# A decoder block on one core: short waits of later stages, and the order of the products in front

## The chip, the cores and the metric

The kernel runs on one core of a Trainium2 chip. Its engines are TensorE (PE in the profile), VectorE (DVE), ScalarE (ACT), GpSimd (POOL) and SyncE (SP), which issues most of the DMAs. Each engine works through its own list of instructions, and semaphores tie the lists together. The metric is the time of one execution on the device in microseconds, the median of several runs.

## What is computed

One layer of a decoder block on a sequence of 1024 positions of width 1024, in float32. Cut to what matters:

```python
mod = silu(c) @ w_ada + b_ada
shift, scale, gate = split(mod, 3)
h = rms_norm(x, norm_gain) * (1 + scale) + shift
q, k, v, z_a, u, z_b, m_a, m_b = split(h @ w_in)
p_a = (stick_breaking_attention(q, k, v) * silu(z_a)) @ w_branch_a
p_b = (multiscale_causal_pool(u, pool_w, pool_scale) * silu(z_b)) @ w_branch_b
merged = sigmoid(m_a) * p_a + sigmoid(m_b) * p_b
y = x + gate * (merged @ w_out)
out = rms_norm(y, final_gain)
```

Attention has 16 heads of 64; each weight is a sigmoid of a logit times the product of (1 - sigmoid) over the later keys before the query. The pooling branch has four groups of 256 channels, each with a trailing window and a linear map of its own.

## The kernel before

**Precision.** A float32 product is made of three products of fp32r operands (a rounded type): operand = high part + low part, and high x high, high x low and low x high are added in one PSUM bank. The high part is a copy into fp32r (`copy_to`, mostly a CAST on ACT), the low part the subtraction operand - high (on DVE as a rule, on POOL for some weights). `load_w` (line 125) loads a weight tile of 512 KB and splits it, `split` (line 110) does the two steps. Product number three of each row block is the first that needs the low part of the weights.

**Stages.** In front, until about 45 us, c goes through silu, the modulation vectors are made on DVE (`modulation`, instructions named mj, 1024 wide, two for each of 8 blocks of h), x is normalised and turned on PE (`square_x`, `scale_x`, `turn_x`) and h is written as high and low (`make_h` on ACT, `low_h` on DVE). Meanwhile PE multiplies the weights of u with the pooling maps (`mapped`: instructions wm, results wg): group g, quarters q 0 to 3. Groups up to `WHOLE` use the plain float32 operands, the later ones fp32r parts. `spread` copies the row c to all partitions with two products with one weight row (crow), and a sigmoid on ACT and a product on DVE give silu(c) there (scb). Then `ua` adds up the first four outputs of u over 8 blocks kb: for each block the eight products with h high (needing `make_h`), later the four with h low (needing `low_h`). Then come v, the pooling branch (wzb, pb), attention with the other projections (z, wt, av, p), and the end, `fin`: for each half `sh` of the sequence eight products pa (attention x w_branch_a, index j), combined on DVE with the gates read back from DRAM (s, m, b: `m*b`, `s<-pa,s`, `m+s`, then high and low parts mhl), then four row blocks o (x w_out), and the last norm (y, qq, t).

**Order.** In front the order is written out by hand: while `pinned` is set, `order(...)` keeps an instruction in the place where the code issues it. Later stages leave the order within an engine to the scheduler of the tile layer, which places instructions by its own estimate of when they can start; so a change of a buffer count can move instructions of a whole stage. PE takes its list in order, and so does DVE: what stands behind a waiting instruction waits too. DMAs of SP are issued in the order of its list, each when its buffer is free. Tags give buffers: `s_`, `m_`, `b_` have 2 each, so a load for index j waits for the user of index j-2. Weights have 2 raw and 2 split buffers (`raw`, `whl`).

**Names.** `ua_273<-hT,wg_143` is output ua from operands hT and wg; numbers behind a name only number buffers. In pa, wa, s, m, b and mhl the digit is the index j.

Of the kernel before, what the change touches and what calls it, by code (L numbers as in the profile page):

```python
# [15 lines left out]
P = 128  # L16
# [20 lines left out]
PLAIN = 8  # L37
LO_V = (1, 0, 1, 1, 0, 1, 1, 0)
# [8 lines left out]
WHOLE, G2 = 2, 1  # L47
# [8 lines left out]
def block_kernel(ctx, tc, a, out):  # L56
# [7 lines left out]
    big = ctx.enter_context(pool("big"))  # L64
    wts = ctx.enter_context(pool("wts"))
# [15 lines left out]
    ident = const.tile([P, P], F32, name="ident")  # L81
    make_identity(nc, ident)
    ones = const.tile([P, P], F32, name="ones")
# [54 lines left out]
    def make_lo(pl, n, tag=None, bufs=3):  # L138

        for _ in range(n):  # L140
# [7 lines left out]
            act.copy(hi, raw)  # L148
            v.tensor_sub(raw.bitcast(F32R), raw, hi.bitcast(F32))
            nc.sync.dma_start(wl_d[i], raw)  # L150

    def load_parts(i, name):
        if i < PLAIN:
            return load_w(a["w_in"][tiles[i]], name, act, gp)
# [47 lines left out]
    with pool("init") as init:  # L202
# [3 lines left out]

        crow = init.tile([P, D], F32, tag="vjunk", bufs=1, name="crow")[0:1]
# [7 lines left out]
        def spread():  # L215
            crows = [bank("tr", f"crow{hf}") for hf in range(2)]
            for hf in range(2):
                mm(crows[hf], ones[0:1, :], crow[:, hf * 512:hf * 512 + 512], start=True, stop=True)
            for hf in range(2):
                sigb = init.tile([P, 512], F32, tag="hf", bufs=2, name=f"sigb{hf}")  # L220
                order(act.activation)(sigb, crows[hf], AF.Sigmoid)
                order(v.tensor_mul)(scb[:, hf * 512:hf * 512 + 512], crows[hf], sigb)
# [18 lines left out]
        def square_x(sb):  # L241
# [3 lines left out]
            gp.tensor_tensor(st[:, 2:3], st[:, 0:1], mhalf[:, 0:1], op=ALU.pow)  # L245

# [33 lines left out]

        def turn_x(sh, kb):
            pt = xts[sh, kb] = bank(("tr", "av")[kb % 2], f"xt{sh}_{kb}")
            for i in range(4):
                transpose(pt[:, i * P:(i + 1) * P], xs[4 * sh + i][:, kb * P:(kb + 1) * P])
# [19 lines left out]
        wg, maps, halves = {}, {}, {}  # L304
# [11 lines left out]
        def split_map(g):  # L316
            hl = init.tile([P, 2, 2, 256], F32R, tag="phl", bufs=1, name=f"phl{g}")
            order(act.copy)(hl[:, 0], maps[g])
            order(v.tensor_sub)(hl[:, 1], maps[g], hl[:, 0].bitcast(F32))
            maps[g] = hl  # L320
# [7 lines left out]
        def mapped(g, q, tag):  # L328
# [4 lines left out]
            th, ml = halves[g, q // 2], maps[g]  # L333
            for e in range(2):
                ks = slice((2 * q + e) % 4 * P, (2 * q + e) % 4 * P + P)

                pairs = [(th[:, cb, ks], ml[:, cb]) for cb in range(2)] if g < WHOLE else [
                    (th[:, i, cb, ks], ml[:, j, cb]) for i, j in ((0, 0), (0, 1), (1, 0)) for cb in range(2)]
                for n, (l, r) in enumerate(pairs):
                    mm(ps[:, e * 256:e * 256 + 256], l, r, start=n == 0, stop=n == len(pairs) - 1)  # L340

            def out(which=(0, 1)):
# [3 lines left out]
                if 1 in which:  # L346
                    order(v.tensor_sub)(dst[:, 1], ps, dst[:, 0].bitcast(F32))
            return out
# [16 lines left out]
        load_mod(0, [slice(1, 2)])  # L365
        load_half(1, 1, t1[:, 1])
        load_x(3)
        load_mod(1)
# [23 lines left out]
        m11 = mapped(1, 1, "pj")  # L392
        modulation(0, (1,))
# [688 lines left out]
```

## Time and profile before

| what | value |
|---|---|
| median of 3 runs | 1212.78 us (1212.56 to 1213.09) |
| the profiled execution, its own time | 1212.4 us |
| its span, first to last instruction | 1210.4 us |
| PE busy | 1199.6 us, 99% of the span |
| DVE, ACT, POOL busy | 757.9, 540.6, 193.8 us |
| mean granted TensorE clock | 0.999 |

PE busy and the span differ by 10.8 us, and the time outside the span is 2.0 us. The profile's timeline gives for each run of equal instructions the start, the time from the first start to the last end, the engine, line and operation, output<-inputs, shapes and count, and in brackets the idle time of that engine before it with what ended it. Ends of PE instructions are modelled: a row block's 512 columns are listed as 0.39 us long but follow one another faster.

### The profile page before, as it was taken

How to read it: one execution, taken by the hardware profiler on the slowest of the kernel's cores; microseconds unless marked ns; L12 is line 12 of the kernel's file. 1: busy time of each engine (PE TensorE's matmuls, PEld its weight loads, DVE VectorE, ACT ScalarE, POOL GpSimd, SP SyncE). 2: the span in 40 equal slices, each digit the busy share in tenths (PEclk: the TensorE clock that was granted, in tenths of full speed). 3: DMA queues.
4: the chain of work that ended last, by engine and by line, in shares of the span. 5: the costliest groups of instructions: out<-in, count | busy, mean ns of one | idle time of the engine just before them, and what ended most of it. 6: DMA issues, size and time to landing. Idle time of an engine off the chain costs nothing.

```text
span 1210.4 us, 16174 instructions
## 1 busy us (share of the span) xinstructions
PE 1199.6 (99%) x5746; PEld 1000.1 (83%) x5746; DVE 757.9 (63%) x1049; ACT 540.6 (45%) x1008; POOL 193.8 (16%) x361
## 2 busy tenths in 40 slices
PE   8999999999999999999999999999999999999997
PEld 7888888888888888888888888888888888888886
DVE  6764482677410277767768677776777763785643
ACT  5564341334211265665556655655655653232211
POOL 1000000001222343212212122231211310000001
PEclk9999999999999999999999999999999999999999
DMA  9649994626846632442635325353343236984622
GB/s 361 255 168 339 326 383 167 214 82 230 317 148 117 179 92 75 133 121 78 170 109 157 113 80 153 109 158 115 106 132 102 96 126 211 315 275 168 218 65 84
DMA packets 81955, 207.13 MB, mean 171 GB/s; under 512 B 10450, under 2 KB 23890, under 8 KB 79699
## 3 DMA queue, kind: packets, MB, share of 16 engines
q1 hardware_dynamic: 73666, 191.23, 49.2%
q10 hardware_dynamic: 8208, 14.88, 3.3%
q8 instruction: 45, 0.74, 0.2%
q14 instruction: 36, 0.29, 0.1%
HBM read 138.96 MB, written 50.34 MB: 156 GB/s over the span
## 4 chain that ended last, share of the span: by engine, by line
PE 93%; DVE 2%; DMA 2%; issue 1%; ACT 0%; POOL 0%; SPq 0%; POOLq 0%; DVEq 0%; ACTq 0%
PE p L99 36%; PE pb L99 7%; PE wzb L99 7%; PE v L99 7%; PE o L99 6%; PE av L99 6%; PE z L99 6%; PE wt L99 5%; PE pa L99 5%; PE u L99 5%; PE ua L99 3%; PE wm L99 1%; DMA m<-sb_d 1%; DMA out_y<-y 0%; DMA praw<-in_pool_w 0%
## 5 line engine op out<-in xcount | busy, mean ns | idle before, releaser
L99 PE MATMUL p<-hT,w 128*128 128x512 f32 x1920 | 480.9, 392 | 0.0
L99 PEld LDWEIGHTS p<-hT,w 128*128 128x128 f32 x1920 | 354.8, 188 | 68.6
L804 DVE TENSOR_TENSOR_SCAN om<-om 128x512 f32<-128x512 f32 (+7 forms) x128 | 175.4, 1370 | 50.0 <-ACT om L797 41.5
L824 DVE TENSOR_TENSOR wt<-wt,wt 128x512 fp32r<-128x512 f32 (+1 forms) x160 | 100.5, 628 | 93.7 <-ACT wt L823 93.1
L823 ACT CAST wt<-wt 128x512 fp32r<-128x512 f32 (+1 forms) x160 | 87.5, 547 | 130.2 <-PE wt L99 129.7
L797 ACT ACTIVATE om<-z 128x512 f32<-128x512 f32 (+2 forms) x192 | 94.9, 494 | 77.2 <-PE z L99 52.2
L802 POOL TENSOR_SCALAR_AFFINE_SELECT om<-om 128x128 f32<-128x128 f32 x128 | 50.9, 397 | 364.3 <-ACT om L797 344.0
L99 PE MATMUL av<-wt,vv 128*128 128x512 f32 x320 | 106.0, 412 | 0.0
L99 DVE TENSOR_TENSOR be<-be,om 128x511 f32<-128x511 f32 (+7 forms) x128 | 95.8, 758 | 0.3
L798 ACT ACTIVATE be<-z 128x512 f32<-128x512 f32 (+2 forms) x192 | 94.2, 491 | 0.0
L99 PE MATMUL pa<-ga,wa 128*128 128x512 f32 x384 | 89.9, 390 | 0.3 <-DVE s L976 0.2
L99 PEld LDWEIGHTS wt<-ident,be 128*128 128x128 f32 x576 | 72.7, 140 | 20.9
L99 PE MATMUL o<-wo,mhl 128*128 128x512 f32 (+1 forms) x408 | 89.6, 377 | 0.0
L99 PE MATMUL wt<-ident,be 128*128 128x128 f32 x576 | 88.7, 272 | 0.0
L99 PE MATMUL v<-wv,hT 128*128 128x512 f32 x384 | 87.2, 389 | 0.0
L99 PE MATMUL wzb<-hT,wzb 128*128 128x512 f32 x384 | 87.2, 389 | 0.0
L99 PE MATMUL pb<-gb,wb 128*128 128x512 f32 x384 | 87.2, 389 | 0.0
L99 PEld LDWEIGHTS o<-wo,mhl 128*128 128x128 f32 x408 | 73.5, 188 | 14.1
L99 PEld LDWEIGHTS pa<-ga,wa 128*128 128x128 f32 x384 | 71.9, 188 | 15.9 <-issue 0.6
L99 PEld LDWEIGHTS v<-wv,hT 128*128 128x128 f32 x384 | 72.1, 188 | 14.9
L99 PEld LDWEIGHTS wzb<-hT,wzb 128*128 128x128 f32 x384 | 72.1, 188 | 14.9
L99 PEld LDWEIGHTS pb<-gb,wb 128*128 128x128 f32 x384 | 72.1, 188 | 14.9
(129 smaller groups left out, 1374.2 us busy)
## 6 DMA issues: line engine op xcount, KB each, us to landing
w_raw<-in_w_in SPq DMA_DIRECT2D x40, 512.0 KB, 4.8
l_raw<-in_w_in SPq DMA_DIRECT2D x32, 512.0 KB, 5.1
wl_d<-l_raw SPq DMA_DIRECT2D x32, 512.0 KB, 5.8
w<-wl_d SPq DMA_DIRECT2D x32, 512.0 KB, 3.9
v_d<-vo SPq DMA_DIRECT2D x16, 512.0 KB, 4.8
vv<-v_d SPq DMA_DIRECT2D x8, 1024.0 KB, 5.5
wa_raw<-in_w_branch_a SPq DMA_DIRECT2D x16, 512.0 KB, 4.8
wa<-in_w_mod SPq DMA_DIRECT2D x7, 1024.0 KB, 6.5
```

What stands on the lines that cost most here:

```text
L99: ins = op(*args, **kw)
L797: act.activation(om[:, b0:b0 + n], zp[:, :n], AF.Sigmoid, scale=-0.125)
L798: act.activation(be[:, b0:b0 + n], zp[:, :n], AF.Sigmoid, scale=0.125)
L802: gp.affine_select(out=tl[:, :P], in_=tl[:, :P], pattern=[[1, P]], compare_op=ALU.is_gt, fill=fill, base=0, channel_multiplier=-1)
L804: v.tensor_tensor_scan(om[:, :W], om[:, :W], om[:, :W], 1.0, ALU.mult, ALU.min)
L823: act.copy(wt[:, 0, :off], pt[:, :off])
L824: v.tensor_sub(wt[:, 1, :off], pt[:, :off], wt[:, 0, :off].bitcast(F32))
```

## The change

1. Front. `ident` and `ones` get a pool of their own, which moves them in memory. A sigmoid on a tile of 8 columns runs first on ACT, with the tile set again by POOL. `spread` is split in two halves, each between `mapped` quarters; quarters 2 and 3 of group 0 use fp32r parts (`WHOLE` is now a table of halves), for which the map and the second half of the weights are split (`cast_map`, `low_map`, `cast`). The scaling of row block 0 goes from DVE to ACT (`scale_act`). The half (1,1) of the weights and x block 3 are loaded ahead of the second half of the first modulation weights. Quarters 2 and 3 of group 1 use banks "av" and "tr", the latter with its second part behind the turning of x, and their low parts come later.
2. The low part of one weight tile of attention (number 4, `MASKED`) goes from POOL to DVE.
3. In the v stage the work on weights to be stored and on the pooling differences is issued one step later than its loads (`later`, `load_u`). The rows of every engine stand there as before.
4. In `fin` the buffers of s, m and b go from 2 to 3.

```diff
-WHOLE, G2 = 2, 1
+WHOLE = ((0, 0), (1, 0), (1, 1))
+MASKED = 4
...
     def load_parts(i, name):
         if i < PLAIN:
-            return load_w(a["w_in"][tiles[i]], name, act, gp)
+            return load_w(a["w_in"][tiles[i]], name, act, v if i == MASKED else gp)
...
+        act.activation(mhalf, mhalf, AF.Sigmoid)
+        gp.memset(mhalf, -0.5)
...
+        def scale_act(sb):
+            order(act.mul)(xs[sb], xs[sb], stats[sb][:, 2:3])
...
         load_mod(0, [slice(0, 1)])
         load_x(2)
-        load_mod(0, [slice(1, 2)])
         load_half(1, 1, t1[:, 1])
         load_x(3)
+        load_mod(0, [slice(1, 2)])
...
-        mapped(0, 0, "pj")()
+        m00 = mapped(0, 0, "pj")
+        cast_map(0)
+        low_map(0)
+        m00()
+        t0_lo = cast(0, 1)
+
+        spread(0)
         m01 = mapped(0, 1, "pj")
+        t0_lo()
+        silu_row(0)
         m01(hi)
         square_x(0)
         m01(lo_)
-        spread()
-        scale_x(0)
+        spread(1)
+        silu_row(1)
+        scale_act(0)
...
         m11 = mapped(1, 1, "pj")
+        m11()
         modulation(0, (1,))
...
-        m11()
-        m12 = mapped(1, 2, "z")
-        m13 = mapped(1, 3, "z")
+        for kb in range(2):
+            bank_x(0, kb)
+        m12 = mapped(1, 2, "av")
+        m13 = mapped(1, 3, "tr", (0,))
         square_x(3)
+        m12(hi)
...
         turn_x(0, 1)
-        m12()
         make_h(0, 0, None)
+        m13.products((1,))
         m13(hi)
         modulation(1)
         load_mod(4)
         low_h(0, 0, v)
+        m12(lo_)
         m13(lo_)
...
-                s_ = fin.tile([P, 512], F32, tag="s_", bufs=2, name=f"s{sh}_{j}")
+                s_ = fin.tile([P, 512], F32, tag="s_", bufs=3, name=f"s{sh}_{j}")
...
-                m_ = fin.tile([P, 512], F32, tag="m_", bufs=2, name=f"m{sh}_{j}")
+                m_ = fin.tile([P, 512], F32, tag="m_", bufs=3, name=f"m{sh}_{j}")
...
-                b_ = fin.tile([P, 512], F32, tag="b_", bufs=2, name=f"b{sh}_{j}")
+                b_ = fin.tile([P, 512], F32, tag="b_", bufs=3, name=f"b{sh}_{j}")
```

**What it moves: DVE in front.** From the silu row (scb) to the scaling of x block 3, before:

```order
L99 TENSOR_TENSOR scb<-crow_163,sigb_169 128x512
L99 TENSOR_SCALAR x_113<-x_113,st_157 128x1024
L99 TENSOR_TENSOR wg_143<-wm_2_173,wg_143 128x512
L99 SCALAR_TENSOR_TENSOR mj_0_190,acc_189<-wa_133,scb 128x1024
L99 TENSOR_TENSOR mods<-acc_189,vecs 128x1
L99 TENSOR_SCALAR x_114<-x_114,st_180 128x1024
L99 TENSOR_TENSOR wg_143<-wm_3_184,wg_143 128x512
L99 TENSOR_TENSOR wg_196<-wm_0_197,wg_196 128x512
L99 TENSOR_SCALAR x_115<-x_115,st_202 128x1024
L99 SCALAR_TENSOR_TENSOR mj_1_214,acc_189<-wa_133,scb 128x1024
```

The same place after, with the three rows ahead of it:

```order
L103 TENSOR_TENSOR wt_1_161<-wt_1_raw,wt_1_161 128x1024
L103 TENSOR_TENSOR scb<-crow_117,sigb_170 128x512
L103 TENSOR_TENSOR wg_150<-wm_1_164,wg_150 128x512
L103 TENSOR_TENSOR scb<-crow_118,sigb_180 128x512
L103 TENSOR_TENSOR wg_150<-wm_2_184,wg_150 128x512
L103 SCALAR_TENSOR_TENSOR mj_0_217,acc_216<-wa_140,scb 128x1024
L103 TENSOR_TENSOR mods<-acc_216,vecs 128x1
L103 TENSOR_SCALAR x_121<-x_121,st_199 128x1024
L103 TENSOR_TENSOR wg_150<-wm_3_203,wg_150 128x512
L103 TENSOR_TENSOR wg_223<-wm_0_224,wg_223 128x512
L103 TENSOR_SCALAR x_122<-x_122,st_229 128x1024
L103 TENSOR_TENSOR wg_223<-wm_1_236,wg_223 128x512
```

The scaling of the first x block (x_113) is gone from DVE; a low part of the map and one of the weights (wt_1) stand ahead of scb.

**DVE in fin, first half of the sequence**, around the low part of wa_3, before:

```order
L123 CAST mhl_1_9541<-m_1_9509 128x512
L114 TENSOR_TENSOR wa_3_9588<-wa_3_raw,wa_3_9588 128x1024
L114 TENSOR_TENSOR mhl_1_9541<-m_1_9509,mhl_1_9541 128x512
L948 TENSOR_TENSOR wor_9628<-wor_9628,bg 128x1024
L948 TENSOR_TENSOR wor_9675<-wor_9675,bg 128x1024
L950 TENSOR_TENSOR wo<-wor_9628,wo 128x1024
L114 TENSOR_TENSOR wa_4_9635<-wa_4_raw,wa_4_9635 128x1024
L950 TENSOR_TENSOR wo<-wor_9675,wo 128x1024
L976 TENSOR_TENSOR s_2_9549<-pa_2_9556,s_2_9549 128x512
```

and after:

```order
L1015 TENSOR_TENSOR m_2_9578<-m_2_9578,b_2_9580 128x512
L127 CAST mhl_1_9568<-m_1_9536 128x512
L118 TENSOR_TENSOR mhl_1_9568<-m_1_9536,mhl_1_9568 128x512
L1022 TENSOR_TENSOR s_2_9576<-pa_2_9583,s_2_9576 128x512
L118 TENSOR_TENSOR wa_3_9615<-wa_3_raw,wa_3_9615 128x1024
L994 TENSOR_TENSOR wor_9655<-wor_9655,bg 128x1024
L1023 TENSOR_TENSOR m_2_9578<-m_2_9578,s_2_9576 128x512
L118 TENSOR_TENSOR wa_4_9662<-wa_4_raw,wa_4_9662 128x1024
```

The low part of wa_3 stood five rows of work ahead of `s_2<-pa_2`, and now stands right behind it. On PE the products pa_3 follow pa_2 without others between in both.

**DVE in fin, second half**, around the low part of wa_2, before:

```order
L1003 TENSOR_TENSOR y_10074<-o_1_10106,y_10074 128x512
L976 TENSOR_TENSOR s_0_10145<-pa_0_10152,s_0_10145 128x512
L977 TENSOR_TENSOR m_0_10147<-m_0_10147,s_0_10145 128x512
L114 TENSOR_TENSOR wa_2_10226<-wa_2_raw,wa_2_10226 128x1024
L1011 SCALAR_TENSOR_TENSOR qq_10076<-qq_10076 128x1
```

and after:

```order
L1049 TENSOR_TENSOR y_10101<-o_1_10133,y_10101 128x512
L1022 TENSOR_TENSOR s_0_10172<-pa_0_10179,s_0_10172 128x512
L1057 SCALAR_TENSOR_TENSOR qq_10103<-qq_10103 128x1
L1023 TENSOR_TENSOR m_0_10174<-m_0_10174,s_0_10172 128x512
L1065 SCALAR_TENSOR_TENSOR y_10101<-y_10101,qq_10103,fg 128x512 x2
L118 TENSOR_TENSOR wa_2_10253<-wa_2_raw,wa_2_10253 128x1024
```

The norm's row factor qq and the two products y of row block 3 came behind the low part of wa_2, and now stand ahead of it. On PE, between the last product o and pa_2 there, five products of pa_0 and eight of pa_1 stand after the change, where two and ten stood before.

## Rows read from the trace of the kernel before

**Rows 1.** The page's part 4, the chain that ended last: shares by engine.

```profile
PE 93%; DVE 2%; DMA 2%; issue 1%; ACT 0%; POOL 0%; SPq 0%; POOLq 0%; DVEq 0%; ACTq 0%
```

**Rows 2.** Waits of PE between 20 and 30 us: total, times, longest.

```profile
PE ua L99 <- ACT hT L99: 1.1, 1, 1.1
PE ua L99 <- DVE wg L99: 1.0, 1, 1.0
```

**Rows 3.** Timeline of the front: start, us, engine, what, shapes, count [idle before].

```profile
10.24 1.06 ACT L99 ACTIVATE junk<-x 128x1025 f32<-128x1025 f32 x1
...
11.41 1.28 ACT L99 ACT_TABLE_LOAD   x1
...
12.71 1.09 ACT L99 ACTIVATE sigb<-crow 128x512 f32<-128x512 f32 x2
13.34 1.29 DVE L99 TENSOR_TENSOR scb<-crow,sigb 128x512 f32<-128x512 f32 x2 [2.26 <-ACT sigb L99]
...
14.54 0.74 DVE L99 TENSOR_SCALAR x<-x,st 128x1024 f32<-128x1024 f32 x1
...
15.80 1.22 DVE L99 SCALAR_TENSOR_TENSOR mj<-wa,scb 128x1024 f32<-128x1024 f32 x1
...
21.67 0.88 DVE L99 TENSOR_SCALAR x<-x,st 128x128 f32<-128x128 f32 x2
...
24.15 1.66 PE L99 MATMUL ua<-hT,wg 128*128 128x512 f32 x6 [1.08 <-ACT hT L99]
...
26.81 0.73 PE L99 MATMUL ua<-hT,wg 128*128 128x512 f32 x2 [1.00 <-DVE wg L99]
...
30.43 0.62 ACT L99 CAST hT<-hf 128x512 fp32r<-128x512 f32 x1
```

**Rows 4.** Timeline at 31.5 us: the products that follow that cast.

```profile
31.25 2.01 PE L99 MATMUL ua<-hT,wg 128*128 128x512 f32 x8
```

**Rows 5.** Timeline in attention, 426 to 433 us.

```profile
426.85 2.40 POOL L114 TENSOR_TENSOR w<-w_raw,w 128x1024 fp32r<-128x1024 f32 x1 [0.20 <-ACT w L119]
...
429.53 1.02 DVE L804 TENSOR_TENSOR_SCAN om<-om 128x384 f32<-128x384 f32 x1 [2.39 <-POOL om L802]
...
430.46 1.54 PE L99 MATMUL p<-hT,w 128*128 128x512 f32 x6
...
432.39 0.50 PE L99 MATMUL z<-kh,q 128*128 128x512 f32 x1 [0.38 <-ACT be L798]
```

**Rows 6.** Timeline in fin, first half of the sequence.

```profile
1033.75 16.93 PE L99 MATMUL pa<-ga,wa 128*128 128x512 f32 x74
...
1039.84 0.69 DVE L976 TENSOR_TENSOR s<-pa,s 128x512 f32<-128x512 f32 x1 [1.20 <-PE pa L99]
```

**Rows 7.** Timeline in fin, second half, at 1124 us.

```profile
1123.96 8.23 PE L99 MATMUL pa<-ga,wa 128*128 128x512 f32 x34
1124.16 0.69 DVE L1003 TENSOR_TENSOR y<-o,y 128x512 f32<-128x512 f32 x1 [4.75 <-PE o L99]
...
1124.77 0.68 DVE L976 TENSOR_TENSOR s<-pa,s 128x512 f32<-128x512 f32 x1
...
1126.10 1.22 DVE L114 TENSOR_TENSOR wa<-wa_raw,wa 128x1024 fp32r<-128x1024 f32 x1
...
1127.23 0.15 DVE L1011 SCALAR_TENSOR_TENSOR qq<-qq 128x1 f32<-128x1 f32 x1
...
1127.37 4.64 PEld L99 LDWEIGHTS pa<-ga,wa 128*128 128x128 f32 x21 [0.49 <-DVE wa L114]
1127.46 0.66 POOL L1014 TENSOR_TENSOR qq<-qq,mhalf 128x1 f32<-128x1 f32 x1 [6.88 <-DVE qq L1011]
...
1129.97 1.41 DVE L1019 SCALAR_TENSOR_TENSOR y<-y,qq,fg 128x512 f32<-128x512 f32 x2
```

**Rows 8.** Timeline in fin, second half, at 1156 us.

```profile
1156.13 0.69 DVE L969 TENSOR_TENSOR m<-m,b 128x512 f32<-128x512 f32 x1 [3.12 <-DMA m<-sb_d]
...
1157.57 0.70 PE L99 MATMUL pa<-ga,wa 128*128 128x512 f32 x2 [0.21 <-DVE s L976]
```

More of the change, by code (lines that the diff above doesn't have):

```diff
@@ L79, in block_kernel @@
     wl_d = dram.tile([5 * KB, P, D], F32, name="wl_d")
-    ident = const.tile([P, P], F32, name="ident")
+    ident = idp.tile([P, P], F32, name="ident")
     make_identity(nc, ident)
-    ones = const.tile([P, P], F32, name="ones")
+    ones = idp.tile([P, P], F32, name="ones")
     gp.memset(ones, 1.0)
@@ L136, in block_kernel, with make_lo @@
     early_lo = iter(range(PLAIN, len(tiles)))
-    def make_lo(pl, n, tag=None, bufs=3):
+    def make_lo(pl, n, tag=None, bufs=3, later=False):
+        rest = []
         for _ in range(n):
@@ L214, in block_kernel, with spread, silu_row @@
             mm(idle[:, :P], ones, ident, start=True, stop=True)
[L215 to L222, printed above, removed]
+        crows = [bank("tr", f"crow{hf}") for hf in range(2)]
+        def spread(hf):
+            mm(crows[hf], ones[0:1, :], crow[:, hf * 512:hf * 512 + 512], start=True, stop=True)
+        def silu_row(hf):
+            sigb = init.tile([P, 512], F32, tag="hf", bufs=2, name=f"sigb{hf}")
+            order(act.activation)(sigb, crows[hf], AF.Sigmoid)
+            order(v.tensor_mul)(scb[:, hf * 512:hf * 512 + 512], crows[hf], sigb)
         mods = init.tile([P, KB, 2], F32, name="mods")
@@ L279, in block_kernel, with bank_x @@
         xts = {}
+        def bank_x(sh, kb):
+            xts[sh, kb] = bank(("tr", "av")[kb % 2], f"xt{sh}_{kb}")
         def turn_x(sh, kb):
-            pt = xts[sh, kb] = bank(("tr", "av")[kb % 2], f"xt{sh}_{kb}")
+            if (sh, kb) not in xts:
+                bank_x(sh, kb)
+            pt = xts[sh, kb]
             for i in range(4):
@@ L332, in mapped, with products @@
             ps = bank(tag, f"wm{g}_{q}")
[L333 to L340, printed above, removed]
+            th = halves[g, q // 2]
+            whole = (g, q // 2) in WHOLE
+            ml = maps[g] if whole else parts_m[g]
+            def products(es):
+                for e in es:
+                    ks = slice((2 * q + e) % 4 * P, (2 * q + e) % 4 * P + P)
+                    pairs = [(th[:, cb, ks], ml[:, cb]) for cb in range(2)] if whole else [
+                        (th[:, i, cb, ks], ml[:, j, cb]) for i, j in ((0, 0), (0, 1), (1, 0)) for cb in range(2)]
+                    for n, (l, r) in enumerate(pairs):
+                        mm(ps[:, e * 256:e * 256 + 256], l, r, start=n == 0, stop=n == len(pairs) - 1)
+            products(es)
             def out(which=(0, 1)):
@@ L347, in out @@
                     order(v.tensor_sub)(dst[:, 1], ps, dst[:, 0].bitcast(F32))
+            out.products = products
             return out
@@ L548, in make_d @@
         nc.sync.dma_start(u[:, :S], u_d[j])
+        return u
+    def make_d(j, u):
+        win = WINDOWS[j // 2]
         cur, n, step = u, S + 16, 1
@@ L598, in block_kernel @@
                 )
-                make_lo(vp, LO_V[sb])
+                now, todo = todo, make_lo(vp, LO_V[sb], later=True)
                 if 8 * hf + sb in DIFFS:
-                    make_d(DIFFS[8 * hf + sb])
+                    j = DIFFS[8 * hf + sb]
+                    todo.append(lambda j=j, u=load_u(j): make_d(j, u))
+                for f in now:
+                    f()
+        assert not todo
     with pool("pb") as pb:
```

53 lines of the change are left out of this document (27 added, 26 removed).

## Prediction

> **What bounds the kernel now.** I read the shares of the chain that ended last first: PE carries 93% of it, and no other engine or DMA more than 2% [rows 1]. So a change pays only where PE itself stands still, or where it is given more or less work. The waits of PE come next. Two stand in the front: 1.1 us before the first product ua, for the cast of h, and 1.0 us in the middle of that first round, for a low part on DVE that empties a bank [rows 2, 3]. Three small ones are left in the later stages, at 432, 1127 and 1157 us [rows 5, 7, 8]. That is all there is to win; the rest of PE's time is its products. One product of 512 columns costs (16.93 - 0.39) / 73 = 0.227 us from start to start [rows 6]. PE and DVE take their lists in order. So the question is which DVE row stands ahead of what PE needs, and there the order of the changed kernel says more than the diff.
>
> **The front.** The first ua needs x block 3 scaled, turned and cast. On DVE the rows from the first mj (15.80) to that scaling (21.67) follow one another with nothing idle and are the same in both kernels, so the scaling moves as the first mj moves [rows 3]. Ahead of it the scaling of x block 0 leaves DVE: -0.74 us. The two new low parts, of the map (512 columns, 0.69 us like the sum y in [rows 7]) and of the weights (1024 columns, 1.22 us [rows 7]), make 1.91 us, and DVE idled 2.26 us before scb [rows 3]: I take them as hidden, at nothing, and if that cover is gone they cost up to 1.9. So the first ua comes about 0.7 us sooner. The second wait (1.0 us) ends by the change of banks: the fourth ua no longer needs a bank that DVE has to empty. PE would so be 1.7 us ahead. It can't keep all of it. Its next inputs are made by a DVE that gained only 0.7: the cast of h for block 2 ends at 31.05, and its products start at 31.25 + 3 x 0.227 = 31.93, which leaves 0.88 us of slack [rows 3, 4]. So 0.7 + 0.88 = 1.6 is the most at that point, and other steps up to 45 us hang on the same DVE. I take **-1.2**. The ends: -2.1, if both waits go whole (1.1 and 1.0 [rows 2]) and the later inputs keep up; -0.3, if the first ua comes 0.6 us later than I think and what is left is used up by the later casts. PE's own work in front hardly changes: two quarters go to another form, and the weight of crow is changed once more.
>
> The table load that the change removes on ACT lasted 1.28 us, from 11.41 to 12.69, and the sigmoid began at 12.71 [rows 3]. In my sum it is worth nothing of its own: the sigmoid is then waited for no more, but mj stands behind other work. The Trainium skill, page "ScalarE: Activation LUTs", section "What ACT_TABLE_LOAD costs", adds to a load of 1283 ns a drain of 1380 ns, 2.66 us per switch. The load agrees; of a drain the trace shows nothing, as 0.02 us passed. By the page's price the front would gain up to 1.4 us more and the sum below would come to -0.3 us, which is still within 0.2%.
>
> **The low part of weight tile 4.** POOL held it for 2.40 us, so the mask of om came late, the scan on DVE began at 429.53 after 2.39 idle, and z, due at 430.46 + 6 x 0.227 = 431.82, began at 432.39 [rows 5]: 0.57 us. On DVE the low part costs 1.22 [rows 7] in time that it idled, so the scan starts about 1.2 us sooner and the wait is gone: **-0.6**; between -0.6 and -0.2, if half of the 2.39 us were needed otherwise.
>
> **The later v stage** moves no row: 0, and I see nothing that it could cost.
>
> **fin: the waits that go.** At 1127 the third product of pa_2 is the fifteenth from 1123.96, due at 1123.96 + 14 x 0.227 = 1127.13; it came at 1127.37 [rows 7]. With 0.1 us more at its restart: **-0.3**. But this wait is replaced by another, below. At 1157 pa waits for s, queued behind m*b, which had waited 3.12 us for its load [rows 8]. The load waited for a buffer; with three buffers it is issued an index earlier, and in the new order s stands ahead of the next m*b: **-0.4** (the 0.21 of the row, and 0.2 as the row at 432 showed 0.38 idle where 0.57 was lost). Its ends are -0.4 and 0.
>
> **fin: the waits that come.** DVE rows have been moved, and two of the moved rows wait for PE.
> First half: the low part of wa_3 now stands right behind s_2<-pa_2, which needs the last product of pa_2. The 74 products from 1033.75 are two of pa_0 and 24 each of pa_1, pa_2 and pa_3 [rows 6]. The last of pa_1 starts at 1033.75 + 25 x 0.227 = 1039.42, and s_1 at 1039.84, 0.42 later. The last of pa_2 starts at 1044.85, so s_2 at 1045.27. The next DVE row begins 0.61 later (1124.16 to 1124.77 [rows 7]), at 1045.88, the low part takes 1.22, and PE goes on 0.05 after it (1126.10 + 1.22 = 1127.32, PE at 1127.37 [rows 7]): 1047.15. PE wants it at the third product of pa_3, 1033.75 + 52 x 0.227 = 1045.53. So **+1.6**. Before, the same low part was made while pa_2 ran.
> Second half: the low part of wa_2 now stands behind s_0, qq, m+s and the two products y, and y waits for POOL. Five products of pa_0 follow the last o: the fifth starts at 1123.96 + 4 x 0.227 = 1124.87, s_0 at 1125.29, qq 0.61 later at 1125.90, POOL's step 0.23 after that (1127.23 to 1127.46 in [rows 7]) and 0.66 long, to 1126.79. Then y x2 for 1.41, the low part 0.08 before its end (rows overlap by that), at 1128.2, ready at 1129.4. The third product of pa_2 is now the sixteenth, due at 1127.36. So **+2.0**.
> Both come from the list alone and from durations that hardly vary, so the ends are near: 1.0 to 1.8 for the first, 1.2 to 3.0 for the second (less if the last product o ends later than the rest, more if ACT's square, which qq needs, is late).
>
> **The sum.** -1.2 - 0.6 - 0.3 - 0.4 + 1.6 + 2.0 = +1.1 us. On the profiled execution, 1212.4, that is 1213.5; it lies 0.4 below the median of the runs shown, so on the median 1212.78 + 1.1 = **1213.9 us**. A measurement of this kernel can tell about 0.2% (2.4 us) from no change, so "the same" is 1210.4 to 1215.2, and 1213.9 lies in it.
>
> **Rivals.**
> *The new waits don't come.* If DVE reaches the low parts of wa_2 and wa_3 in time after all, 3.6 us go from the sum: 1213.9 - 3.6 = 1210.3, faster by just over 0.2%. For it: the diff only adds buffers there, and the scheduler chose this order by its own estimates. Against it: DVE waited 4.75 us for o with the low part of wa in its list behind it [rows 7], so it does not overtake. 12%.
> *ACT becomes the bound of the front.* Ahead of quarter 2's cast ACT is given the cast of the map (0.62 like the cast of h), of the weights (1.06, as the 1025 columns of junk) and the scaling of x block 0 (1.06), and loses 1.28: +1.46 us [rows 3]. If the first mj hangs on that cast, the first ua comes up to 1.4 us later instead of 0.7 sooner; with the second wait gone (-1.0) the front is worth +0.4 and the sum +2.7: 1215.5, slower. It decides from the point where the front loses over 0.1 us. For it: the low part of quarter 2 stands directly ahead of the first mj. Against it: mj stood behind the scaling that now leaves DVE, and DVE's idle 2.26 us were spent waiting for ACT's sigmoid, which no longer has the table load ahead of it [rows 3]. 25%.
> *The mask stays late* at 432 us because DVE has the low part in its way: +0.6 on the sum, 1214.5, the same verdict. 8%.
>
> **Chances.** My forecast 55%, with the late mask 63% for the same, 12% faster, 25% slower. The range takes the ends of the parts: below, -2.1 - 0.6 - 0.3 - 0.4 + 1.0 + 1.2 = -1.2, 1211.6; above, it takes in most of the slower case, 1215.5 with the second new wait somewhat longer, 1216.2.
>
> **What would show it.** In the profile after: the first ua at about 23.4 and no wait of PE for DVE at 25 to 27, but short ones between 28 and 44; no wait for z at 432; a wait of pa for DVE wa of about 1.6 us near 1046 and one of about 2 us near 1126; none at 1156. The prediction is wrong if PE's list runs through pa_3 and pa_2 without those two, or if the front gains or loses over 2 us.

## The result, and the profile after

The changed kernel takes 1216.43 us, the median of 9 runs (1215.78 to 1217.53), the kernel before 1213.06 us in the same set of runs. The ratio is 1.003, with a 95% interval from 1.002 to 1.004: slower by 0.3%, 3.4 us. The prediction was 1213.9 us with a range up to 1216.2 and "the same" as the likeliest case. So the time lies 0.2 us above the range, and the likeliest case was not the one that came. The kernel before stood 0.28 us higher in this set of runs than in the three on which the prediction built; as a difference, +3.4 us stands against a forecast of +1.1 and an upper end of +3.4.

The waits of PE, after (total us, times, longest):

```profile
PE pa L103 <- DVE wa L118: 3.7, 2, 2.2
PE xt L103 <- DVE x L103: 0.8, 1, 0.8
...
PE ua L103 <- ACT hf L103: 0.3, 1, 0.3
PE ua L103 <- DVE hT L103: 0.2, 1, 0.2
```

Against [rows 2] the two waits of the front are gone from their places, but PE now waits 0.8 us a little earlier, at xt (the turning of x block 3), for DVE's scaling of that block, and 0.5 us at two later blocks of h: 1.3 us of waits where 2.1 stood. The small wait for z in attention is gone [rows 5], and two new ones stand in fin, both for the low part of wa. Where the time went is read from the starts of the same PE instructions in both traces, after minus before. At the norms behind the front (75 us) it is +0.70. Past the former wait for z it is +0.07. It drifts up to +0.50 through attention, is +4.46 right behind the two new waits, and +4.00 at the end, past the place of the former wait at 1157. The spans differ by the same 4.0 (1214.4 and 1210.4). The two waits that went had cost 0.34 us (at 1127) and 0.45 (at 1157): the product that waited came 0.23 and 0.37 late, and the one behind it 0.1 more. The same slower restart is in the new waits. The term by term account:

| term | predicted | traced | |
|---|---|---|---|
| front | -1.2 | +0.70 | a start that came 0.85 late by chance, and a front 0.15 shorter, see the front |
| low part of tile 4 | -0.6 | -0.66 | |
| attention, second half of the projections | none | +0.43 | not foreseen |
| fin, waits that go (1127, 1157) | -0.7 | -0.79 | |
| fin, new wait for wa_3 | +1.6 | +1.78 | 1.62 the wait, the rest the restart |
| fin, new wait for wa_2 | +2.0 | +2.51 | 2.40 the wait, the rest the restart |
| sum | +1.1 | +4.0 | +3.1 with the starts made equal |

**The two new waits.** Timeline of the first, PE and DVE (start, us, engine, what, shapes, count [idle before]):

```profile
1045.79 0.69 DVE L1022 TENSOR_TENSOR s<-pa,s 128x512 f32<-128x512 f32 x1 [0.94 <-PE pa L103]
...
1046.39 1.22 DVE L118 TENSOR_TENSOR wa<-wa_raw,wa 128x1024 fp32r<-128x1024 f32 x1
...
1047.66 2.58 PE L103 MATMUL pa<-ga,wa 128*128 128x512 f32 x10 [1.46 <-DVE wa L118]
```

The low part starts 0.60 us behind the start of s, and PE goes on 1.87 behind it; the prediction had 0.61 and 1.88. (In the list before, six rows stood between that low part and s_2, where five were counted.) The second, in the other half:

```profile
1126.02 3.56 PE L103 MATMUL pa<-ga,wa 128*128 128x512 f32 x15
...
1127.35 0.69 DVE L1022 TENSOR_TENSOR s<-pa,s 128x512 f32<-128x512 f32 x1 [0.44 <-PE pa L103]
1127.96 0.15 DVE L1057 SCALAR_TENSOR_TENSOR qq<-qq 128x1 f32<-128x1 f32 x1
...
1128.19 0.98 POOL L1060 TENSOR_TENSOR qq<-qq,mhalf 128x1 f32<-128x1 f32 x1 [5.55 <-DVE qq L1057]
...
1129.21 1.41 DVE L1065 SCALAR_TENSOR_TENSOR y<-y,qq,fg 128x512 f32<-128x512 f32 x2 [0.44 <-POOL qq L1060]
...
1130.54 1.22 DVE L118 TENSOR_TENSOR wa<-wa_raw,wa 128x1024 fp32r<-128x1024 f32 x1
...
1131.82 3.48 PE L103 MATMUL pa<-ga,wa 128*128 128x512 f32 x14 [2.24 <-DVE wa L118]
```

The row that begins at 1131.82 was due behind fifteen products, at 1126.02 + 15 x 0.227 = 1129.43, so 2.39 us are lost. The chain is the predicted one, s, qq, POOL, y, wa. Its POOL step took 0.98 us where the row before had 0.66 [rows 7], and that is most of the difference from 2.0. DVE stood still for 0.44 us in it, with PE waiting for the row behind.

**The wait that went**, at 1157: PE runs through, where [rows 8] had a wait for s.

```profile
1155.74 0.69 DVE L1022 TENSOR_TENSOR s<-pa,s 128x512 f32<-128x512 f32 x1 [0.95 <-PE pa L103]
1157.67 0.69 DVE L1015 TENSOR_TENSOR m<-m,b 128x512 f32<-128x512 f32 x1 [1.24 <-DMA m<-sb_d]
```

As the order said, s stands ahead of the next m*b, so the 1.24 us that m*b still waits for its load hold up nobody.

**The front.** DVE, ACT and POOL, to be held against [rows 3]:

```profile
14.24 1.15 ACT L103 ACTIVATE x<-x,st 128x1024 f32<-128x1024 f32 x1 [0.26 <-POOL st L262]
...
15.30 0.56 ACT L103 CAST wg<-wm 128x512 fp32r<-128x512 f32 x1
...
15.90 0.69 DVE L103 TENSOR_TENSOR wg<-wm,wg 128x512 fp32r<-128x512 f32 x1 [1.19 <-ACT wg L103]
...
16.50 1.21 DVE L103 SCALAR_TENSOR_TENSOR mj<-wa,scb 128x1024 f32<-128x1024 f32 x1
...
18.16 0.75 DVE L103 TENSOR_SCALAR x<-x,st 128x1024 f32<-128x1024 f32 x1 [0.24 <-POOL st L262]
...
22.68 0.88 DVE L103 TENSOR_SCALAR x<-x,st 128x128 f32<-128x128 f32 x2
```

The first mj starts at 16.50, 0.70 later than before, though a scaling left DVE. The low part of quarter 2 ahead of it waited 1.19 us for ACT's cast, and that cast stands behind the scaling that ACT now does, which itself waited for a step on POOL. The scaling of x block 3 comes at 22.68 instead of 21.67, and the first ua at 24.87 instead of 24.15. PE behind it:

```profile
30.84 3.40 PE L103 MATMUL ua<-hT,wg 128*128 128x512 f32 x12 [0.17 <-DVE hT L103]
...
45.12 2.11 PE L103 MATMUL ua<-hT,wg 128*128 128x512 f32 x8 [0.31 <-ACT hf L103]
```

The twelve products that take 3.40 us take 3.01 where nothing stalls them (the row at 30.93 of the kernel before has the same twelve), so 0.4 are lost inside. With the 0.8 us at xt, these short waits use up what the removed 1.0 us wait had given.

### The profile page after: what moved, and what is told of

The parts are those of the page before. It is cut to its first block, busy times and chain, and to the rows that moved or that the text cites. A ratio compares the mean times of both kernels' runs of the same rounds, so it can differ in the third digit from the quotient of the medians.

```text
span 1214.4 us, 16181 instructions
## 1 busy us (share of the span) xinstructions
PE 1201.4 (99%) x5754; PEld 1000.3 (82%) x5754; DVE 761.8 (63%) x1051; ACT 542.9 (45%) x1011; POOL 193.2 (16%) x361
## 4 chain that ended last, share of the span: by engine, by line
PE 95%; DVE 2%; issue 1%; DMA 1%; ACT 1%; POOL 0%; POOLq 0%; DVEq 0%; ACTq 0%
PE p L103 36%; PE pb L103 7%; PE wzb L103 7%; PE v L103 7%; PE pa L103 7%; PE o L103 6%; PE z L103 6%; PE av L103 6%; PE wt L103 5%; PE u L103 5%; PE ua L103 2%; PE wm L103 1%; DMA wa<-in_w_mod 1%; DVE mj L103 1%; PE idle L103 0%
## 5 line engine op out<-in xcount | busy, mean ns | idle before, releaser
L848 POOL TENSOR_SCALAR_AFFINE_SELECT om<-om 128x128 f32<-128x128 f32 x128 | 53.6, 419 | 365.2 <-ACT om L843 346.5
```

Source lines behind the costliest of these rows:

```text
L848: gp.affine_select(out=tl[:, :P], in_=tl[:, :P], pattern=[[1, P]], compare_op=ALU.is_gt, fill=fill, base=0, channel_multiplier=-1)
```

## The experiments

Medians stand beside those of the kernel before on the same chip. Those of before were 1212.76, 1212.84, 1212.89 and 1212.75 us in the four groups of runs, 21 to 28 runs each.

### fin: are the buffers alone the cause?

**fin_only**, the kernel before with this edit alone:

```diff
-    s_ = fin.tile([P, 512], F32, tag="s_", bufs=2, ...)
+    s_ = fin.tile([P, 512], F32, tag="s_", bufs=3, ...)
-    m_ = fin.tile([P, 512], F32, tag="m_", bufs=2, ...)
+    m_ = fin.tile([P, 512], F32, tag="m_", bufs=3, ...)
-    b_ = fin.tile([P, 512], F32, tag="b_", bufs=2, ...)
+    b_ = fin.tile([P, 512], F32, tag="b_", bufs=3, ...)
```

> The kernel before with 3 instead of 2 buffers for s, m and b in fin, nothing else. Theory (the buffers alone reorder DVE, and the low parts of wa stand behind rows that wait for PE): PE waits 1.6 us for the low part of wa_3 near 1046 and 2.0 to 2.4 us for that of wa_2 near 1126, the old waits there and at 1157 (0.3 and 0.4) are gone, so +3.0 to +3.3 us over before. Rival (the new order of fin came from the moved front, or the waits are hidden without it): 0 to -0.8 us.

Measured: 1218.47 us (1217.31 to 1219.37, 5 runs), ratio 1.0045 [1.003, 1.0059]. Both waits are there, 1.62 and 2.40 us lost. So the buffers alone bring them, by the new order of DVE's list. But the kernel is 5.7 us slower, 2.2 more than the new waits less those that went (3.5). The stretch from 1132 to 1136 us, in fin_only and then in the changed kernel (us, then busy time and count of PE, PEld, DVE, ACT, POOL; granted clock, DMA share, GB/s):

```profile
1132.00:1136.00 4.00, 4.00 (x12) 3.18 (x11) 3.74 (x6) 0.00 (x0) 0.00 (x0) 0.58 0.72 254
```

```profile
1132.00:1136.00 4.00, 4.00 (x18) 3.29 (x19) 3.93 (x7) 0.00 (x0) 0.00 (x0) 1.00 0.86 241
```

And the 24 products that follow the wait, in the same two:

```profile
1131.40 7.37 PE L99 MATMUL pa<-ga,wa 128*128 128x512 f32 x24 [2.23 <-DVE wa L114]
```

```profile
1131.82 5.75 PE L103 MATMUL pa<-ga,wa 128*128 128x512 f32 x24 [2.24 <-DVE wa L118]
```

After the same wait the granted clock falls to 0.58 in the one and stays at 1.00 in the other. In fin_only eight products run at 427 ns instead of 227, and the 24 take 1.62 us more.

**fin_again**, the same kernel once more, asks whether that fall belongs to it.

> fin_only once more, for a second profile. Theory (after the 2.4 us wait PE's clock falls to its lower level in most executions of it, 427 instead of 227 ns for some eight products): the slow products are there again, the time 1217 to 1219. Rival (chance in that one profile): none, and about 1216.

Measured: 1218.77 us (1217.39 to 1218.88, 3 runs), ratio 1.0041 [1.0026, 1.0056]. The fall is there again, eight products at 427 ns.

**m_only**, three buffers for m alone, s and b left at two:

```diff
-    m_ = fin.tile([P, 512], F32, tag="m_", bufs=2, ...)
+    m_ = fin.tile([P, 512], F32, tag="m_", bufs=3, ...)
```

> The kernel before with 3 buffers for m alone, s and b keep 2. In its list the low parts of wa_3 (first half) and of wa_2 (second half) stand ahead of the rows that wait for the next pa. Theory (order on DVE, not the number of buffers, makes the new waits): no wait of pa for DVE wa, the one at 1157 us for s gone, -0.4 to -0.8 us. Rival (three buffers delay the loads of wa and with them the low parts): waits of 1 us and more for wa as in fin_only, +1 to +3 us.

Measured: 1212.31 us, ratio 0.9998 [0.9989, 1.0007]. Of its fin no wait of pa for wa is left and none at 1157. On DVE, at the place of the first new wait:

```profile
1045.14 0.69 DVE L114 TENSOR_TENSOR mhl<-m,mhl 128x512 fp32r<-128x512 f32 x1
1045.74 1.22 DVE L114 TENSOR_TENSOR wa<-wa_raw,wa 128x1024 fp32r<-128x1024 f32 x1
```

The low part of wa_3 stands ahead of s_2 again. So one buffer more for m takes the waits at 1127 and 1157 away (0.82 us in the trace) without the two new ones. The time doesn't show it. The profiled execution hides it too: it lost 1.86 us at pb near 309, in a wait of a kind that comes and goes (see the end).

### Tile 4

**masked_only**, the kernel before with the low part of weight tile 4 on DVE:

```diff
-    return load_w(a["w_in"][tiles[i]], name, act, gp)
+    return load_w(a["w_in"][tiles[i]], name, act, v if i == 4 else gp)
```

> The kernel before with the low part of weight tile 4 on DVE instead of POOL. Theory: the wait for z at 432 us is gone, -0.6 us, nothing else moves. Rival (DVE is late with it): 0 or more, with a wait for z left.

Measured: 1212.40 us, ratio 0.9993 [0.9983, 1.0002]. In the trace the wait for z is gone and 0.66 us with it, as in the changed kernel. The time agrees in sign but can't be told from no change; the profiled execution also lost 1.1 us at u near 83, in a wait that comes and goes.

### The front

**front_only**, the changed kernel with parts 2 and 4 undone:

```diff
-    return load_w(a["w_in"][tiles[i]], name, act, v if i == MASKED else gp)
+    return load_w(a["w_in"][tiles[i]], name, act, gp)
...
-    s_, m_, b_: bufs=3   # the three lines of fin, shortened
+    s_, m_, b_: bufs=2
```

> The changed kernel with 2 buffers for s, m and b and the low part of tile 4 on POOL again, so the front and the later v stage alone. Theory (ACT bounds the front: square, scaling of x block 0 and the casts stand ahead of quarter 2's cast and of the next square, so x block 3 is scaled 1.0 us later): PE is 0.7 us later than before at the norms (75 us), the time +0.7 us. Rival (PE's clock rose late in that one execution by chance, which cost 0.9 us): with an early rise the front is -0.2 us or better.

Measured: 1213.52 us (1212.71 to 1215.85, 10 runs), ratio 1.0006 [0.9997, 1.0015]. The front, which should have won 1.2 us, wins nothing that the time could show; the move in memory, below, is in it.

**front_dve**, front_only with the scaling of x block 0 back on DVE, tells whether ACT is the reason:

```diff
-        scale_act(0)
+        scale_x(0)
```

> front_only with the scaling of x block 0 on DVE again, as before; all else of the new front stays. Theory (on ACT that scaling stands ahead of quarter 2's cast and of the square of x block 1, 1.15 us each time): the first mj starts near 15.8 instead of 16.5, the scaling of x block 3 near 21.7 instead of 22.7, and the time is about 0.7 to 1.0 us under front_only's. Rival (the wait lies with the late rise of PE's clock or with PE's apart crow products, not with ACT): the same as front_only, 0.0 to 0.2 us.

Measured: 1212.58 us, ratio 0.9997 [0.9987, 1.0006]. **front_noid** is front_only with `ident` and `ones` back in their old place (below, under memory):

```diff
-    ident = idp.tile([P, P], F32, name="ident")
+    ident = const.tile([P, P], F32, name="ident")
-    ones = idp.tile([P, P], F32, name="ones")
+    ones = const.tile([P, P], F32, name="ones")
```

> front_only with ident and ones in the pool of constants again. Between 400 and 1040 us PE lost 0.4 to 0.5 us in steps too small to see in each execution of the new front (after, after_again, front_only) and none in fin_only and masked_only. Theory (the move of ident and ones in memory does it): the loss over that stretch is gone, under 0.1 us against the kernel before. Rival (something else of the new front or chance): it is 0.4 to 0.5 us again.

Measured once, 1212.51 us. Between these profiles the first products of the span differ, although the lists are the same. The first eight wm products, in the changed kernel and in **front_noid_t**, a copy of front_noid that was timed later:

```profile
6.03 2.82 PE L103 MATMUL wm<-praw,wt_raw 128*128 128x256 f32 x8
```

```profile
6.19 1.96 PE L103 MATMUL wm<-praw,wt_raw 128*128 128x256 f32 x8
```

In the changed kernel three of the gaps between them are 427 ns, in the other all but the first are 216. That is the factor between the two levels of the clock, 1.2 and 2.4 GHz. The clock column shows 1.00 for the stretch in both, but the clock's record in the trace begins only at 7.83 us in the one and at 5.90 in the other, and the last slow gap of the changed kernel ends at 7.80. In some executions the first product also waits up to 0.7 us for its load. The eighth product starts between 7.57 and 8.71 us in 17 of the 18 profiles, with the old front and the new (7.62 in before, 7.71 in fin_only, 8.51 in banks_late), so this start belongs to the execution and not to the change. In the profile of front_only all eight were slow and the eighth came at 10.02, which is why nothing is read of the front from it. Fronts can be compared only at an equal start.

> front_noid, timed: the new front with ident and ones at their old place. Theory (of front_only's +0.8 us, 0.4 is the move in memory, the rest ACT): +0.2 to +0.5 us against before. Rival (the front itself is the whole loss): +0.8.

Measured: 1213.54 us (1211.81 to 1214.69), ratio 1.0004 [0.9995, 1.0014]. The time can't tell it from no change. Its profile starts nearly as fast as that of before, its eighth product 0.15 us later:

```profile
13.54 1.15 ACT L103 ACTIVATE x<-x,st 128x1024 f32<-128x1024 f32 x1 [0.26 <-POOL st L262]
...
15.80 1.22 DVE L103 SCALAR_TENSOR_TENSOR mj<-wa,scb 128x1024 f32<-128x1024 f32 x1
...
21.99 0.87 DVE L103 TENSOR_SCALAR x<-x,st 128x128 f32<-128x128 f32 x2
```

The first mj starts at 15.80, as before [rows 3]; the scaling of x block 3 is 0.32 late and the first ua comes at 24.17 (24.15 before). The norms start at 74.70, before at 74.66. With the 0.15 us of the start taken off, the new front is worth -0.1 us. The same stretch of front_dve, whose start was the earliest of all:

```profile
13.12 0.69 DVE L103 TENSOR_TENSOR scb<-crow,sigb 128x512 f32<-128x512 f32 x1 [0.80 <-ACT sigb L103]
...
13.73 0.74 DVE L103 TENSOR_SCALAR x<-x,st 128x1024 f32<-128x1024 f32 x1
...
15.05 1.23 DVE L103 SCALAR_TENSOR_TENSOR mj<-wa,scb 128x1024 f32<-128x1024 f32 x1
...
20.12 1.59 POOL L262 TENSOR_TENSOR st<-st,mhalf 128x1 f32<-128x1 f32 x1 [2.01 <-ACT junk L103]
...
21.75 0.88 DVE L103 TENSOR_SCALAR x<-x,st 128x128 f32<-128x128 f32 x2 [0.18 <-POOL st L262]
```

With the scaling on DVE the first mj does come 0.75 us sooner. Yet the scaling of x block 3 comes at 21.75, no sooner than before: it now waits for POOL's row factor, which waited for ACT's square. The first ua is at 23.95, the norms at 74.48. So behind the wait for ACT's cast stood a second bound, ACT's square and POOL's step, which took 1.59 us here and 0.81 in before.

**front_dve_noid** repeats the comparison with `ident` and `ones` in their old place.

> The same with the scaling of x block 0 on DVE. Theory: 0.4 to 0.9 us under front_noid_t, so -0.3 to -0.6 us against before. Rival (ACT's share is small): as front_noid_t.

Measured: 1212.53 us, ratio 0.9996 [0.9987, 1.0005]. Its profile began slowly, with the norms at 75.04; front_noid began slowly as well, with 75.28. What the scaling's place is worth shows when all rows are counted from the start of the eighth product wm (us; best and best_noid are the kernels further down, with the scaling on DVE):

| run | scaling of block 0 | eighth wm | first mj, behind it | norms, behind it |
|---|---|---|---|---|
| before | DVE | 7.62 | 8.18 | 67.04 |
| after | ACT | 8.47 | 8.04 | 66.89 |
| front_noid | ACT | 8.34 | 8.03 | 66.94 |
| front_noid_t | ACT | 7.77 | 8.03 | 66.93 |
| front_dve | DVE | 7.57 | 7.48 | 66.91 |
| front_dve_noid | DVE | 8.46 | 7.42 | 66.58 |
| best | DVE | 8.35 | 7.41 | 66.55 |
| best_noid | DVE | 7.94 | 7.42 | 66.58 |

In the other six profiles of the old front mj comes 8.18 us behind, to 0.01 us, and the norms 66.97 to 67.05. So the new front gains 0.1 us with the scaling on ACT. With it on DVE it gains 0.46 to 0.49 in three of four profiles and 0.13 in front_dve, where POOL's step for x block 3 was the longest (1.59 us, 1.20 to 1.28 in the three). Two things follow. The scaling on ACT costs about 0.35 us at the norms. And mj comes 0.7 us sooner with the scaling of block 0 still ahead of it on DVE, so it is not the leaving of that row that brings mj forward, but the earlier end of scb: 14.63 us in before [rows 3], 13.81 in front_dve. DVE had idled 2.26 us for its sigmoid and now idles 0.8.

**banks_late** is the kernel before with the change of banks alone, which takes away the wait of 1.0 us:

```diff
-        m12 = mapped(1, 2, "z")
-        m13 = mapped(1, 3, "z")
+        for kb in range(2):
+            bank_x(0, kb)
+        m12 = mapped(1, 2, "av")
+        m13 = mapped(1, 3, "tr")
...
-        m12()
+        m12(hi)
...
+        m12(lo_)
```

> The kernel before with quarters 2 and 3 of group 1 in the banks av and tr and their low parts later, nothing else of the new front. Theory (the lead that PE wins by the bank is used up by h inputs that come no sooner): the 1.2 us wait near 25.4 goes, but new short waits for h at 30 to 32 and near 44 us leave -0.3 to -0.4 us at the norms. Rival (the lead stays): -1.2 us.

Measured: 1212.68 us, ratio 0.9998 [0.9989, 1.0007]. PE in front:

```profile
25.03 2.12 PE L99 MATMUL ua<-hT,wg 128*128 128x512 f32 x8 [1.08 <-ACT hT L99]
...
30.71 3.39 PE L99 MATMUL ua<-hT,wg 128*128 128x512 f32 x12
...
44.99 1.20 PE L99 MATMUL ua<-hT,wg 128*128 128x512 f32 x4 [0.25 <-ACT hf L99]
```

The wait in the middle of the first eight products is gone. Its start was a slow one, so the first ua stands 0.88 us later than before. At 30.71 PE is 0.22 ahead of before (30.93), and the rest of the lead goes in the stall inside those twelve products and in the wait at 44.99: at the norms it is 0.70 behind, a lead of 0.88 - 0.70 = 0.18 us (0.19 when counted from the eighth product wm). Removing the second wait of the front was worth 0.2 us, not 1.

### Memory: the drift in attention

From the first product p of the second half of the projections to the first pa, before takes 639.50 us. The changed kernel takes 0.47 more, if what the wait for z gives back is left out (0.69 us over this stretch in masked_only; the +0.43 of the first table counts from just behind z). **before_idp** is the kernel before with `ident` and `ones` in a pool of their own, which leaves the rows of every engine as they are:

```diff
+    idp = ctx.enter_context(pool("idp"))
-    ident = const.tile([P, P], F32, name="ident")
+    ident = idp.tile([P, P], F32, name="ident")
-    ones = const.tile([P, P], F32, name="ones")
+    ones = idp.tile([P, P], F32, name="ones")
```

> The kernel before with ident and ones in a pool of their own, behind the big tile; every engine's list is as before, only ident, ones and the h tile (1 KB lower) lie elsewhere in memory. Theory (the move costs PE 0.4 to 0.5 us in small steps between 400 and 1040 us): +0.4 us, the loss in the same stretch. Rival (it takes the new front as well): no loss there, 0.0.

Measured: 1213.43 us, ratio 1.0003 [0.9994, 1.0012]. In the trace the stretch takes 0.61 us more, 0.13 of it near 415 us, where the others lose 0.05 or nothing, the rest spread as in the changed kernel. **fin_idp** is that edit on top of fin_only, and asks besides whether the places in memory decide the fall of the clock.

> fin_only with ident and ones moved as in the changed kernel. Theory: as fin_only and 0.4 more, 1218 to 1219.5, with the fall of the clock after the second wait. Rival (the places decide): no fall, 1216.2 to 1216.8.

Measured: 1217.16 us (1216.82 to 1219.37), ratio 1.0037 [1.0023, 1.0051]; in the profiled execution (1218.35 us) the clock falls. The median lies 1.3 us below that of fin_only and not 0.4 above; three of its five runs took about 1217 us. The ends of the stretch, in fin_only and then in fin_idp:

```profile
389.35 2.88 PE L99 MATMUL p<-hT,w 128*128 128x512 f32 x12
1028.84 4.47 PE L99 MATMUL pa<-ga,wa 128*128 128x512 f32 x19
```

```profile
389.95 2.43 PE L100 MATMUL p<-hT,w 128*128 128x512 f32 x10
1029.91 3.34 PE L100 MATMUL pa<-ga,wa 128*128 128x512 f32 x14
```

The first takes 639.49 us, the second 639.96, 0.47 more. **after_noid** is the changed kernel with `ident` and `ones` in their old place.

> The changed kernel with ident and ones at their old place; PE's and DVE's lists in fin are the same as in fin_only and in the changed kernel. Theory (places in memory have no say in the clock, only +0.4 us in attention): -0.4 us against the changed kernel, +3.0 to +3.5 against before, no fall of the clock in fin. Rival (the places decide the fall): the clock falls after the second wait as in fin_only, +5 us.

Measured: 1218.50 us (1215.23 to 1219.18, 5 runs), ratio 1.0035 [1.0022, 1.0048]; the clock falls, as its rival said, and the stretch takes no more than before. But in fin_idp, with the moved places, it falls too, so the places do not decide it. Over 17 profiles, with the wait for z and the loss at 415 left out, the seven with the moved tiles are 0.43 to 0.50 us longer in that stretch, and the ten without are within 0.03. That the move causes the loss is shown. Which of the moved places does it, those two tiles themselves or h, which lies 1 KB lower, stays open. The times can't tell half a microsecond; this rests on the traces.

### The changed kernel again, and a better one

**after_again** is the changed kernel in another set of runs.

> The changed kernel once more, beside the others on one chip and for a second profile of its front. Theory: +3.4 us, the sum of the three parts (3.2 + 0.7 - 0.6), and PE's clock rises near 7.9 us again. Rival (the late rise is chance): the clock rises near 5.4 us and the front is 0.9 us shorter in this profile.

Measured: 1216.78 us (1215.82 to 1219.68), ratio 1.0033 [1.0023, 1.0042]. The result stands; its profile shows no fall of the clock.

**best** keeps what the runs above bore out: the changed kernel with the scaling on DVE and three buffers for m alone.

```diff
-        scale_act(0)
+        scale_x(0)
...
-    s_, b_: bufs=3   # the two lines of fin, shortened
+    s_, b_: bufs=2
```

> front_dve, with the low part of tile 4 on DVE and 3 buffers for m alone: what the experiments so far point to. Theory: front -0.3 to 0, tile 4 -0.6, fin -0.7, loss in attention +0.4: -0.9 to -1.2 us against before, -4 to -5 against the changed kernel. Rival (parts don't add up, since the scheduler moves fin again): near 0.

Measured: 1211.26 us (1210.78 to 1213.12, 11 runs), ratio 0.9987 [0.9979, 0.9996]. All waits of PE behind its first instruction in the profile:

```profile
PE xt L103 <- DVE x L103: 0.4, 1, 0.4
PE ua L103 <- ACT hf L103: 0.3, 1, 0.3
PE ua L103 <- DVE hT L103: 0.2, 1, 0.2
```

**best_noid** is best with `ident` and `ones` in their old place.

> The kernel best with ident and ones left in the pool of constants. Theory: the loss of 0.45 us in attention goes, so -0.4 us against best, -1.6 to -2.0 against before. Rival (that loss came with the front): as best.

Measured: 1210.87 us (1210.38 to 1213.44, 11 runs), ratio 0.9985 [0.9976, 0.9994]. Both are faster than the kernel before, by about 0.14%, and than the changed one by 0.4%. The 0.4 us between the two have the size of the loss in attention, but their intervals overlap. The profiled execution of best_noid (1212.72 us) is one of its slow ones: it lost 1.9 us in three waits in the v stage.

## Why the prediction was wrong

**The step that failed is the front.** It was put at -1.2 us and is worth -0.1 (counted from an equal start), the largest miss of the sum. The prediction had two premises there. The first: "the scaling moves as the first mj moves", and mj comes 0.74 us sooner because a scaling leaves DVE. But the row directly ahead of mj, the low part of quarter 2, waits for ACT, and ACT had been given that very scaling: mj came 0.15 us sooner. With the scaling left on DVE mj does come 0.7 sooner, from the earlier sigmoid and not from a row less, and that the two new low parts are hidden was right. Even then the scaling of x block 3 did not move as mj moved: by 0.2 us in three profiles and not at all in front_dve, since ACT's square and POOL's step ended last. "Nothing idle" told only that DVE was the later of two: in before, POOL's step for block 3 ended at 21.30 us and the scaling began at 21.67 [rows 3].

```profile
20.49 0.81 POOL L245 TENSOR_TENSOR st<-st,mhalf 128x1 f32<-128x1 f32 x1 [2.56 <-ACT junk L99]
```

The prediction counted the durations of rows that stood close together on DVE and did not ask of each which producer ended last behind it.

The second premise: about half a microsecond of the 1.0 us of the second wait is kept, out of 0.88 us of slack at block 2. It took 0.4 off for the later steps up to 45 us that hang on the same DVE, without a row for them. banks_late shows it: 0.2 us are left at the norms.

**The rival had the mechanism, not the price.** "ACT becomes the bound of the front" was given 25% and 1215.5 us: the first mj hanging on ACT's cast. That is what the trace shows. But it has the first ua up to 1.4 us later and the second wait worth 1.0; counted from an equal start the first ua came 0.1 sooner and the second wait was worth 0.2, and the front is -0.1 and not its +0.4. That its 1215.5 lies nearer to the measured time than the forecast is luck: what fills the gap is the loss in attention and the longer waits in fin, which it did not have. The reason against it, that the table load is out of ACT's way, was true but overlooked that the cast stands behind the scaling, which waits for POOL.

**The places in memory had no term.** The split of pools was told as part of the change but was not priced; it costs 0.47 us in attention by the traces.

**fin was right in its mechanism, 0.6 us short in size.** Both waits came for the foreseen reason at the foreseen place, the first to 0.02 us; fin_only shows that the buffers alone bring them. The second was 0.4 larger, most of it POOL's step (0.98 for 0.66), and each had a slower restart of 0.1 to 0.2 us that the sum left out. The range for the second, 1.2 to 3.0, held. The waits at 1127 and 1157 went as foreseen (-0.79 for -0.7). Not foreseen was that a wait of that length can be followed by a fall of the clock: another 1.6 us, in some of the executions, and most likely in the slowest runs of the changed kernel (up to 1219.68), though no profile of those was taken.

**The table load** was put at nothing, since the sigmoid would be waited for no more. It is still waited for: DVE idles 0.8 us ahead of the second scb in front_noid_t and front_dve. No run undoes this edit alone. What the load and the split of spread are worth together shows with the scaling left on DVE: mj comes 0.7 us sooner. At the norms the whole front then gains 0.46 to 0.49 in three profiles, where the change of banks alone gave 0.2. So the term was not nothing; the scaling on ACT took most of it back. In the changed kernel ACT's first two rows are the load and the sigmoid on the small tile:

```profile
0.79 1.28 ACT L220 ACT_TABLE_LOAD   x1 [0.79 <-PEq L1120]
2.09 0.21 ACT L220 ACTIVATE mhalf<-mhalf 128x8 f32<-128x8 f32 x1
```

The sigmoid again begins 0.02 us after the load's end, as in [rows 3]. The drain of 1380 ns that the Trainium skill, page "ScalarE: Activation LUTs", section "What ACT_TABLE_LOAD costs", puts on top of a load is not to be seen here either. The gain of 1.4 us more that it would have meant did not come: the whole front gains 0.1, and at most 0.49 with the scaling on DVE.

**Tile 4 was right**: -0.66 for -0.6, and the mask was not late. The v stage shows no term in the two profiles of the changed kernel. But part 3 of the change was never run alone, and four of the ten profiles that have it show a wait of PE for vo there (0.8 to 1.9 us lost in after_noid, front_only, front_dve and best_noid), none of the eight without it. The rows stand in the same order with it and without, so this may be chance; it stays open.

**The sum**, with the runs' values: -0.1 in front, -0.66, +0.43 in attention behind it, and -0.79 + 1.78 + 2.51 in fin, makes +3.2 us; measured were +3.4.

## What to carry to other kernels

Where a row is to come sooner because work left its engine, look at what each row between there and the goal waits for: rows that follow one another without idle time may hide a second producer that ends only a few tenths of a microsecond earlier. A buffer count is a change of order wherever a scheduler places the instructions: one more buffer for m alone took away the waits that three more took away, without two new ones of 4 us together, and only the row ahead of the waiting one on the in-order engine tells them apart. Price every line of a diff that moves tiles in memory as a term of its own, from below and above zero. And before two traces of a front are compared, the same early row is looked up in both, and the difference of their starts taken off.

## What the runs showed of the hardware

**A fall of the clock after a wait.** After 2.4 us in which PE waited in fin, the granted clock fell to its lower level for eight products in four of six profiled executions (fin_only, fin_again, fin_idp, after_noid) and not in the other two (the changed kernel and its copy). It never fell after the wait of 1.6 us. The lists of PE and DVE in fin are the same in all six, and the places in memory don't decide it, since fin_idp and after_noid have it with moved and unmoved tiles. PE was at work again when it fell, for 1.24, 1.04, 0.94 and 0.65 us. By the clock's record in the traces it fell 1126.40 us behind its rise at the start of the execution in all four, while that rise itself came anywhere from 6.24 to 7.62 us. In the other two executions the same distance from the rise ends 2.41 and 2.15 us behind the restart, and nothing fell. So it goes with where the wait lies as counted from the clock's rise; that is read from six profiles, no run tests it, and the cause is not shown.

**A slow start.** In 17 of 18 profiles the eighth product of the span starts between 7.57 and 8.71 us, in one at 10.02, whatever the kernel; slow products (427 ns for 216) and a late first load (up to 0.7 us) make the difference. **Waits that come and go.** Nine of the 18 profiles lost between 0.2 and 1.9 us at u, v or pb, between 80 and 310 us, in waits for rows of DVE or ACT that the other profiles do not have, three of them in kernels whose only edits lie in later stages (masked_only, m_only, fin_again). So one profile's span does not price a change of half a microsecond; its own rows do. **A place in memory** changes the time of a stretch of 640 us by half a microsecond with no instruction moved. **POOL's power** of one column took from 0.55 to 1.59 us; in front and in fin it stands in the chain that PE waits for.
